# One streaming trunk layer on Trainium2: first weight tiles repacked, one small load issued elsewhere, three weight splits and two operand splits re-ordered

## The chip, the cores and the metric

The kernel runs on one core of a Trainium2 chip. The metric is the device time of one execution in microseconds (us). The kernel before takes 1087.67 us, the median of three runs (1087.66 to 1087.76). In the text a difference of 1 us is therefore about 0.09%.

## The reference, cut to what matters

One layer of a streaming encoder serves 512 new tokens (a prompt chunk) and 64 tokens of a running stream at once, 1024 features wide. Three blocks each add to `x`, and a last norm follows:

```python
x += mixer(rmsnorm(x))        # gated delta net (4 heads) and gated linear attention, merged by sigmoid gates, then w_o
x += cross_attn(rmsnorm(x))   # 4 heads of 256, into 256 memory tokens, then w_mo
x += conv_ffn(rmsnorm(x))     # up 1024 -> 2 x 2816, causal conv of width 3, SiLU gate, down
y  = rmsnorm(x)
```

The change touches four places of this: the first projections of the mixer (`q`, `k`, `v` of head 0, each 1024 -> 128, out of the normed `x`, whose per-feature gain is a vector), the product with `w_o` at the mixer's end, the attention output of the last memory head (`softmax(q k^T) v`), and the load of that gain vector. Everything is computed in float32 accuracy.

## The kernel before, in words

**Layout.** Features stand on the 128 partitions and tokens along the free axis: `x` is eight tiles of 128 x 576 (512 and 64 tokens side by side), and a weight tile of 1024 x 128 is one 128 x 1024 tile in the on-chip memory, eight 128 x 128 blocks behind each other.

**Accuracy by two halves.** TensorE takes operands in a rounded format (`fp32r`). Each operand is therefore split into a rounded high part and the rounded remainder, named `xh`, `xl` for the normed `x`, `ach`, `acl` or `hl` for other activations, and two tiles or halves named `w` for a weight. A product is three passes: high x high, weight high x remainder, weight remainder x high. `mm3` emits these for one 128 x 128 block, two matmuls each (256 and 320 tokens, in two PSUM banks `sm`): six matmuls for each block.

**Two ways to split a weight.** The raw weight comes by DMA into a tile `wr` on SyncE's queue. *With the subtraction*: ScalarE casts it to the high part (CAST), and VectorE or GpSimd subtracts the high part from the raw weight (TENSOR_TENSOR w<-wr,w). *Summed* (`split_summed`, L644): ScalarE writes the negated rounded weight into the place of the remainder (ACTIVATE with scale -1) and the high part (CAST), and then a DMA issued by GpSimd adds the raw weight onto the negated one. That DMA reads the raw weight a second time from HBM (`w<-wt`), or, where the weight is a sum of blocks formed on the chip, from that sum's tile `ws` (`w<-ws`).

**Products by sums of blocks.** For `w_o` two neighbouring output tiles form a pair (`WPAIRS`, four pairs, named by their first tile m = 0, 2, 4, 6). Each pair is done with seven products of sums of blocks: P1, P2, Q4, Q5, Q6, P3, Q7. `emit_product` (L651) loads the raw tiles with P1, forms the sums with `total` on VectorE or GpSimd (tiles `ws`), and splits each sum; its line `summed = ...` says which of the products take the summed way. `products` (L1645) emits the matmuls, `product_order` gives their order: pair by pair, with Q4 of a pair put behind P1 and Q5 of the next. The matmuls of a product come as eight with the weight's high part and then four with its remainder (128 x 288 each). `wo_finish` adds a finished bank to the tiles of `x` (SCALAR_TENSOR_TENSOR x<-sm,x on VectorE), and only then is that bank free for the product that accumulates into it next: Q5 and P3 share one bank, and P3 follows Q5 by one product.

**What sets the order.** All of this is written by one Python program. The main generator (`main`, L1689) emits the matmuls in order; other chains (norms, gates, attention heads) are generators beside it. A planner (`Driver`, L251) gives each instruction of the other engines a start time from costs per element (`FIXED`, `PACE`), keeps them in a heap, and `flush` (L289) emits them in the order of the planned times; the call stands in line 292, so that nearly every instruction has that line in the profile. Each engine then works through its own list in order and waits on semaphores. `load` plans a DMA of SyncE's queue, `accumulate` one of GpSimd. A chain that yields a list of tiles goes on when these are planned to be ready; one that yields a tuple of keys waits for other chains. One change in the planned times can so move rows in other places of the lists.

**The start.** SyncE issues the first eight numbers per partition of the gain vector (`vec`, 4 KB) and then tiles of `x` and halves of two raw weight tiles in turn (`WPART`, L760: which half follows which tile of `x`). The first two raw tiles hold `q` and `k` of head 0, packed so that the first holds both for the first four blocks. ScalarE makes `xh` and the weights' high parts, VectorE `xl` and the remainders. TensorE meanwhile runs eleven matmuls on constants (`warm`), then the blocks of `q` and `k`: q of block k and k of block k-1 in each step of the loop over `first2`. Then follow 32 matmuls with `w0` (gates; `sm<-x,w` in the profile), `v` of head 0 with a weight tile of its own, loaded after the others, and `za` (the gate of head 0). Among these are the sum of squares for the norm (`sm<-keep,acc`); from it GpSimd makes the factor `rt`, VectorE the diagonal tiles `dg`, TensorE spreads them (`sm<-dg,onesr`), ScalarE copies the result to `rbc`, VectorE multiplies with it (`ba<-sm,rbc`), and TensorE goes on with `sm<-cst,ba`.

**The attention heads.** `c_att` (L1527) emits one memory head: scores, softmax, transposes of the probabilities (`pth`, `ptl`), and two value products j = 0, 1 of 128 features each (banks `sm<-pth,kvh`). After each of them ScalarE copies the banks to `ao`, and `hl2` splits it into `ach` (ScalarE) and `acl` (VectorE). The output product `mo` of the first two tiles starts with heads 0 to 2, and takes head 3 as soon as its split parts are there.

Of the kernel before, what the change touches and what calls it, by code (L numbers as in the profile page):

```python
# [250 lines left out]
class Driver:  # L251
# [129 lines left out]

    def load(self, out, in_):
        cost = self.FIXED["D"] + free(out) * self.PACE["D"]
        start = self.place("D", max(self.ready_at(out), self.latest(self.seen, out)) + 2.2, cost)
        self.mark(self.wrote, start + cost, [out])
        self.put(start - 2.2, [(self.sync.dma_start, (out, in_), {})])

# [116 lines left out]
def tile_trunk(ctx, tc, xT, memT, wt, wd, vec, cst, w0, wgate, st_gdn, st_conv, st_gla, st_ffn, ckT, cv,  # L504
# [19 lines left out]
    def nm(s):  # L524
        cnt[0] += 1
        return f"{s}{cnt[0]}"
# [30 lines left out]
    def big():  # L557
        return Pair(sm(), sm())
# [41 lines left out]
    def make(i):  # L600
        fn = unmade.pop(i, None)
        if fn is not None:
            fn()
# [47 lines left out]
    def emit_product(i, at, pair, prod):  # L651
# [35 lines left out]
        h, lo = w[:, 0:n], w[:, 512:512 + n]  # L687
        summed = prod in ("P1", "P2", "Q4") or prod == "Q5" and n > 256 and pair[0][0] not in ("wo", "dn")

# [47 lines left out]


    ones_r = cp.tile([P, 128], F32R, name="onesr")
    G.memset(f(ones_r), 1.0)  # L740
# [8 lines left out]

    vec_t = cp.tile([P, NV], F32, name="vec")  # L750
    keep_t = cp.tile([P, 256], F32, name="keep")
    mbc_t = cp.tile([P, 256], F32, name="mbc")
    cst_t = small_tile([P, NM - 256], F32, tag="cst", name="cst", bufs=1)
    DMA(vec_t[:, 0:8], vec[:, 0:8])
    x = []
    raws = [wp.tile([P, 1024], F32, tag="raw", name=nm("wr"), bufs=RAWB) for _ in range(2)]
    for t_ in raws:
        keep(drv.rotate("raw", RAWB, t_))

    WPART = {0: (0, 0, 512), 2: (0, 512, 1024), 3: (1, 0, 512), 5: (1, 512, 1024)}  # L760
    for k in range(KT):
# [765 lines left out]
    def c_att(hd):  # L1527
# [51 lines left out]
        for j in range(2):  # L1579
# [10 lines left out]
            for c, reg in ((slice(0, TP), pp), (slice(TP, T), p64[:, 0:64])):  # L1590
                A.copy(o[:, c], reg)
            yield [o]
            ao[2 * hd + j] = hl2(o)
            os_.append(o)
            yield
        mops[hd] = {p: cut(ao[2 * hd + i], N1) for i, p in enumerate(("P1", "P2"))}
# [17 lines left out]
    def hl2(src, new=None):  # L1614
        h, lo = [(new or slot)(s, F32R) for s in ("ach", "acl")]
        parts2(h[:, 0:T], lo[:, 0:T], src[:, 0:T])
        return h[:, 0:T], lo[:, 0:T]
# [71 lines left out]
    def main():  # L1689
        acc = slot("acc")  # L1690
        xg = []
        for i in range(2):
            wready[i] = (w_tile()[:], w_tile()[:])
# [39 lines left out]
        drop(*(t_[:] for t_ in raws))  # L1733
        emit_weight(2)
        make(2)
        DMA(wg_t, wgate)
        DMA(cst_in, st_conv)
        xs = xs_of(xg)
        b0 = []
        (wh0, wl0), (wh1, wl1) = weight("q", 0, False), weight("k", 0, True, True)  # L1740
        first2 = [big(), big()]
        for k in range(KT + 1):
            for i, ps in enumerate(first2):
                j = k - i
                if 0 <= j < KT:
                    wh, wl = (wh0, wl0) if j < 4 else (wh1, wl1)
                    mm3([(ps[:, 0, 0:256], slice(0, 256)), (ps[:, 1, 0:320], slice(256, T))], wh, wl, *xs[j], 2 * (j % 4) + i, j == 0, j == KT - 1)
        raw_u = [conv_raw(ps, V.tensor_copy) for ps in first2]
        for k in range(4, KT):
# [24 lines left out]

        yield from tile_proj("v", 0, xs, b0)
        u0 = conv_raw(b0[0], A.copy)
        yield from tile_proj("za", 0, xs, b0)
        z0 = slot("z")
        for i, o in pieces(b0[1], z0):
            A.copy(o, i)  # L1780
# [711 lines left out]
def pack_inputs(inp):  # L2492
# [13 lines left out]
    for (kind, idx), i in WIDX.items():  # L2506
# [13 lines left out]
        wt[i] = kp(w)  # L2520
    wt[0:2] = wt[0:2].reshape(2, P, 2, 4, P).transpose(2, 1, 3, 0, 4).reshape(2, P, 1024)
    wd = a["w_down"][0].reshape(NJ, P, 8, P)[sum(PARTK, [])].transpose(2, 1, 0, 3).reshape(8, P, NJ * P)
# [65 lines left out]
```

## Time and profile before

| what | value |
|---|---|
| median of the runs | 1087.67 us (1087.66 to 1087.76) |
| the profiled execution's own time | 1090.06 us |
| its span in the trace | 1088.3 us |
| TensorE busy | 1077.5 us, 99% of the span |
| VectorE, ScalarE, GpSimd busy | 749.4, 705.9, 363.3 us |
| moved by DMA | 172.00 MB, mean 158 GB/s |
| weights added by DMA (`w<-wt`, `w<-ws`) | 153 and 27 of 256 to 512 KB |

The trace comes from one execution, whose own time is 2.39 us above the median of the runs; its span lies 1.76 us below that own time. In the rows, PE is TensorE, PEld its weight loads, DVE VectorE, ACT ScalarE, POOL GpSimd, SP SyncE with its DMA queue. A row of the timeline gives start, duration, engine, output and inputs, and in brackets the idle time just before and what ended it. Buffer numbers are left out of these names. TensorE's matmuls are pipelined, so that each lasts longer than the distance to the next; the distance is what counts. PEclk is the clock that was granted to TensorE, 1.00 being full.

### The profile page before, as it was taken

The numbers are of one execution on the slowest core, as the hardware profiler recorded it, in microseconds if no ns is written. First come the engines' busy times: TensorE is split into PE (matmuls) and PEld (weight loads), VectorE is DVE, ScalarE is ACT, GpSimd is POOL, SyncE is SP. The second block draws the span as 40 slices with busy tenths as digits, with TensorE's granted clock in tenths as the row PEclk, the third lists the DMA queues.
The fourth block names the chain that finished last, engine by engine and source line by source line (L and its number), as shares of the span: only waits on it lengthen the run. The fifth ranks groups of instructions, "written<-read, shape, count | busy, mean of one in ns | idle before, by whom it ended". The sixth has DMA issues, their size and how long they took to land.

```text
span 1088.3 us, 21600 instructions
## 1 busy us (share of the span) xinstructions
PE 1077.5 (99%) x8278; PEld 1045.7 (96%) x8278; DVE 749.4 (69%) x1460; ACT 705.9 (65%) x1404; POOL 363.3 (33%) x578
## 2 busy tenths in 40 slices
PE   9999999999999999999999999999999999999997
PEld 7999989998988999999999999999999999999997
DVE  6566844776757586887735766667877776778565
ACT  6675637464647568566755668768876776677645
POOL 1243216134524433123410125444333333332224
PEclk9999999999999999999999999999999999999999
DMA  9666344354136889678684258777788688778934
GB/s 295 145 143 162 70 110 114 76 123 122 43 78 130 213 213 188 246 222 211 174 221 146 49 124 195 175 166 150 166 195 196 146 213 188 168 172 184 201 77 112
DMA packets 68039, 172.00 MB, mean 158 GB/s; under 512 B 7904, under 2 KB 14176, under 8 KB 67936
## 3 DMA queue, kind: packets, MB, share of 16 engines
q0 software_dynamic: 30672, 71.84, 38.2%
q1 hardware_dynamic: 36976, 98.26, 27.7%
q8 instruction: 65, 1.06, 0.4%
q10 hardware_dynamic: 288, 0.52, 0.1%
q14 instruction: 38, 0.31, 0.1%
HBM read 158.15 MB, written 5.37 MB: 150 GB/s over the span
## 4 chain that ended last, share of the span: by engine, by line
PE 97%; DVE 1%; ACT 1%; DMA 0%; issue 0%; SPq 0%; ACTq 0%; DVEq 0%
PE sm L292 97%; DMA x<-xT 0%; DVE ql L292 0%; ACT w L292 0%; DVE w L292 0%; DVE acl L292 0%; DVE ws L292 0%; ACT ach L292 0%; SPq L292 0%; ACT ao L292 0%; DVE q L292 0%; DVE xl L292 0%; ACT xh L292 0%; DVE yo L292 0%; DVE x L292 0%
## 5 line engine op out<-in xcount | busy, mean ns | idle before, releaser
L292 PE MATMUL sm<-xh,w 128*128 128x290 f32 (+3 forms) x2304 | 446.3, 300 | 0.4 <-ACT xh L292 0.3
L292 PEld LDWEIGHTS sm<-xh,w 128*128 128x128 f32 x2304 | 357.2, 189 | 5.4 <-issue 1.7
L292 PE MATMUL sm<-xl,w 128*128 128x290 f32 (+3 forms) x1152 | 270.7, 296 | 0.5 <-DVE xl L292 0.5
L292 POOL DMA_DIRECT2D w<-wt x153 | 135.4, 898 | 372.4 <-ACT w L292 277.4
L292 PE MATMUL sm<-ach,w 128*128 128x256 f32 (+1 forms) x1216 | 230.9, 295 | 2.2 <-DVE x L292 1.7
L292 PEld LDWEIGHTS sm<-xl,w 128*128 128x128 f32 x1152 | 200.9, 189 | 1.0 <-DVE xl L292 1.0
L292 PEld LDWEIGHTS sm<-ach,w 128*128 128x128 f32 x1216 | 189.9, 188 | 3.0 <-ACT w L292 1.9
L292 ACT CAST w<-wr 128x512 fp32r<-128x512 f32 (+5 forms) x207 | 158.7, 769 | 20.8 <-PE sm L292 17.8
L292 ACT ACTIVATE w<-wr 128x512 fp32r<-128x512 f32 (+5 forms) x186 | 142.8, 769 | 20.4 <-PE sm L292 18.7
L292 PE MATMUL sm<-acl,w 128*128 128x256 f32 (+1 forms) x608 | 146.3, 295 | 0.3 <-DVE acl L292 0.3
L292 ACT CAST w<-ws 128x512 fp32r<-128x512 f32 (+1 forms) x132 | 78.4, 603 | 46.8 <-DVE ws L292 26.2
L292 PEld LDWEIGHTS sm<-acl,w 128*128 128x128 f32 x608 | 107.4, 188 | 0.5 <-DVE acl L292 0.5
L292 DVE TENSOR_TENSOR w<-ws,w 128x512 fp32r<-128x512 f32 (+1 forms) x104 | 76.1, 740 | 19.9 <-ACT w L292 17.7
L292 DVE SCALAR_TENSOR_TENSOR fc<-fu,vec,fc 128x578 f32<-128x578 f32 x88 | 70.4, 815 | 3.0 <-ACT fc L292 2.9
L292 PE MATMUL sm<-sh,w 128*128 128x290 f32 x288 | 61.2, 297 | 0.0
L292 DVE TENSOR_TENSOR x<-x,sm 128x320 f32<-128x320 f32 (+3 forms) x95 | 38.7, 437 | 31.4 <-PE sm L292 31.0
L292 POOL DMA_DIRECT2D w<-wd x33 | 29.0, 898 | 64.8 <-ACT w L292 57.9
L292 ACT ACTIVATE fc<-fu,vec 128x578 f32<-128x578 f32 x44 | 38.1, 871 | 17.0 <-POOL fu L292 16.4
L292 PEld LDWEIGHTS sm<-sh,w 128*128 128x128 f32 x288 | 47.5, 189 | 0.0
L292 DVE TENSOR_TENSOR ws<-ws,wr 128x512 f32<-128x512 f32 (+1 forms) x64 | 44.1, 690 | 1.1
L292 PE MATMUL sm<-oh,w 128*128 128x256 f32 (+1 forms) x256 | 44.7, 295 | 0.0
L292 POOL DMA_DIRECT2D w<-ws x27 | 23.6, 873 | 50.4 <-ACT w L292 49.9
(388 smaller groups left out, 1958.1 us busy)
## 6 DMA issues: line engine op xcount, KB each, us to landing
wr<-wt SPq DMA_DIRECT2D x130, 512.0 KB, 5.8
w<-wt POOLq DMA_DIRECT2D x52, 512.0 KB, 6.5
w<-wt POOLq DMA_DIRECT2D x101, 256.0 KB, 6.3
w<-ws POOLq DMA_DIRECT2D x27, 256.0 KB, 5.7
x<-xT SPq DMA_DIRECT2D x16, 288.0 KB, 6.1
wr<-wd SPq DMA_DIRECT2D x8, 448.0 KB, 5.9
w<-wd POOLq DMA_DIRECT2D x8, 448.0 KB, 7.1
wr<-wt SPq DMA_DIRECT2D x12, 256.0 KB, 3.8
```

What stands on the lines that cost most here:

```text
L292: fn(*args, **kw)
```

## The change

It has four parts.

1. `load` takes an issuer. The load of `vec[:, 0:8]` is issued by ScalarE's queue as its first instruction (ahead of its table load), no longer as the first of SyncE's queue.
2. `q`, `k` and `v` of head 0 share the first three raw tiles. They are packed block by block (q, k, v of block 0, then of block 1, and so on: 24 blocks in three tiles), and arrive in six halves behind tiles 0, 1, 2, 3, 5 and 6 of `x`. For each tile of `x` TensorE does the block of q, of k and of v. The own load and split of v's weight is gone (its summed split had an accumulating DMA, which goes with it), and the next weights (`za`) are fetched after these loops. The `w0` matmuls, the sum of squares and `za` follow directly; v's banks are copied by ScalarE.
3. `emit_product` takes the summed way also for Q5 of the pairs m = 2, 4, 6 of `w_o`. These three remainders are no longer subtracted by VectorE or GpSimd, but made by a second ScalarE instruction and an accumulating DMA out of the tile `ws`.
4. In head 3 of the attention the two value products are both emitted, and copied to `ao`, before either output is split by `hl2`.

```diff
-    def load(self, out, in_):
+    def load(self, out, in_, issuer=None):
...
-        self.put(start - 2.2, [(self.sync.dma_start, (out, in_), {})])
+        self.put(start - 2.2, [((issuer or self.sync).dma_start, (out, in_), {})])
...
-        summed = prod in ("P1", "P2", "Q4") or prod == "Q5" and n > 256 and pair[0][0] not in ("wo", "dn")
+        summed = prod in ("P1", "P2", "Q4") or prod == "Q5" and n > 256 and (pair[0][0] not in ("wo", "dn") or pair[0][0] == "wo" and pair[0][1])
...
+    vec_t = cp.tile([P, NV], F32, name="vec")
+    DMA(vec_t[:, 0:8], vec[:, 0:8], nc.scalar)
...
-    vec_t = cp.tile([P, NV], F32, name="vec")
...
-    DMA(vec_t[:, 0:8], vec[:, 0:8])
...
-    raws = [wp.tile([P, 1024], F32, tag="raw", name=nm("wr"), bufs=RAWB) for _ in range(2)]
+    raws = [wp.tile([P, 1024], F32, tag="raw", name=nm("wr"), bufs=RAWB) for _ in range(3)]
...
-    WPART = {0: (0, 0, 512), 2: (0, 512, 1024), 3: (1, 0, 512), 5: (1, 512, 1024)}
+    WPART = {k: (n // 2, 512 * (n % 2), 512 * (n % 2) + 512) for n, k in enumerate((0, 1, 2, 3, 5, 6))}
...
-            yield [o]
-            ao[2 * hd + j] = hl2(o)
             os_.append(o)
+            if not (hd == 3) or j:
+                yield [o]
+            for i in (range(2) if j and (hd == 3) else () if (hd == 3) else (j,)):
+                ao[2 * hd + i] = hl2(os_[i])
...
-        for i in range(2):
+        for i in range(3):
             wready[i] = (w_tile()[:], w_tile()[:])
...
-        emit_weight(2)
-        make(2)
...
-        (wh0, wl0), (wh1, wl1) = weight("q", 0, False), weight("k", 0, True, True)
-        first2 = [big(), big()]
-        for k in range(KT + 1):
-            for i, ps in enumerate(first2):
-                j = k - i
-                if 0 <= j < KT:
-                    wh, wl = (wh0, wl0) if j < 4 else (wh1, wl1)
-                    mm3([(ps[:, 0, 0:256], slice(0, 256)), (ps[:, 1, 0:320], slice(256, T))], wh, wl, *xs[j], 2 * (j % 4) + i, j == 0, j == KT - 1)
-        raw_u = [conv_raw(ps, V.tensor_copy) for ps in first2]
+        ws = [weight(kd, 0, False, i) for i, kd in enumerate("qkv")]
+        first3 = [big() for _ in range(3)]
+        for k in range(KT):
+            for i, ps in enumerate(first3):
+                n, b = divmod(3 * k + i, 8)
+                mm3([(ps[:, 0, 0:256], slice(0, 256)), (ps[:, 1, 0:320], slice(256, T))], *ws[n], *xs[k], b, k == 0, k == KT - 1)
+        raw_u = [conv_raw(ps, copy) for ps, copy in zip(first3, (V.tensor_copy, V.tensor_copy, A.copy))]
+        fetch(3)
...
-        yield from tile_proj("v", 0, xs, b0)
-        u0 = conv_raw(b0[0], A.copy)
+        u0 = raw_u[2]
...
-    wt[0:2] = wt[0:2].reshape(2, P, 2, 4, P).transpose(2, 1, 3, 0, 4).reshape(2, P, 1024)
+    wt[0:3] = wt[0:3].reshape(3, P, KT, P).transpose(2, 0, 1, 3).reshape(3, 8, P, P).transpose(0, 2, 1, 3).reshape(3, P, 1024)
```

TensorE has the same 7340 rows before and after; they stand in another order in three places. At the start, rows 6 to 11 of its list before (sm39/sm40 are q's banks, sm41/sm42 k's; xh17 is tile 0 of the normed x, xh19 tile 1; w13, w14 the first weight's two parts):

```order
L292 MATMUL sm39_131<-xh17_109,w14_106 128x256
L292 MATMUL sm40_132<-xh17_109,w14_106 128x320
L292 MATMUL sm39_131<-xh19_111,w13_105 128x256
L292 MATMUL sm40_132<-xh19_111,w13_105 128x320
L292 MATMUL sm39_131<-xl20_112,w13_105 128x256
L292 MATMUL sm40_132<-xl20_112,w13_105 128x320
```

and with the change (xh20 is tile 0 now; sm43/sm44 are v's banks):

```order
L292 MATMUL sm39_131<-xh20_112,w15_107 128x256
L292 MATMUL sm40_132<-xh20_112,w15_107 128x320
L292 MATMUL sm41_133<-xh20_112,w14_106 128x256
L292 MATMUL sm42_134<-xh20_112,w14_106 128x320
L292 MATMUL sm41_133<-xl21_113,w14_106 128x256
L292 MATMUL sm42_134<-xl21_113,w14_106 128x320
L292 MATMUL sm41_133<-xh20_112,w15_107 128x256
L292 MATMUL sm42_134<-xh20_112,w15_107 128x320
L292 MATMUL sm43_135<-xh20_112,w14_106 128x256
L292 MATMUL sm44_136<-xh20_112,w14_106 128x320
```

Where q went on to tile 1 after six matmuls, q, k and v now all use tile 0 first, 18 matmuls.

In the product with `w_o`, GpSimd's list while pair 0 is being finished, before (w1169 is P1 of pair 2, w1178 Q4 of pair 0, w1182 P2 of pair 2, w1190 and w1191 P1 and Q5 of pair 4; w1176 is Q5 of pair 2):

```order
L292 DMA w1169_6121<-wt 128x512
L292 DMA w1178_6182<-wt 128x512
L292 DMA w1182_6202<-wt 128x512
L292 TENSOR_TENSOR ws1185_6223<-ws1180_6184,wr1167_6119 128x512
L292 DMA w1190_6304<-wt 128x512
L292 DMA w1196_6325<-wt 128x512
L292 DMA w1200_6354<-wt 128x512
```

and with the change:

```order
L292 DMA w1169_6123<-wt 128x512
L292 DMA w1178_6184<-wt 128x512
L292 DMA w1182_6204<-wt 128x512
L292 DMA w1176_6182<-ws1177_6183 128x512
L292 DMA w1196_6328<-wt 128x512
L292 DMA w1190_6287<-wt 128x512
L292 DMA w1200_6354<-wt 128x512
L292 DMA w1191_6313<-ws1192_6314 128x512
```

The addition ws1185 has left GpSimd, and two accumulating DMAs for Q5 weights (w1176, w1191) have come in behind others. VectorE's list in the same place, before (w1179 is Q6 of pair 2, ws1185 the sum for its P3; the two rows behind it add finished banks to `x`, the second of them Q5 of pair 0):

```order
L292 TENSOR_TENSOR ws1180_6184<-ws1177_6181,wr1167_6119 128x512
L292 TENSOR_TENSOR w1176_6180<-ws1177_6181,w1176_6180 128x512
L292 TENSOR_TENSOR w1179_6183<-ws1180_6184,w1179_6183 128x512
L292 SCALAR_TENSOR_TENSOR x1113_5839<-sm1181_6185,x1113_5839 128x288
L292 SCALAR_TENSOR_TENSOR x1114_5840<-sm1183_6203,x1114_5840 128x288
```

and with the change:

```order
L292 TENSOR_TENSOR ws1180_6186<-ws1177_6183,wr1167_6121 128x512
L292 SCALAR_TENSOR_TENSOR x1113_5841<-sm1181_6187,x1113_5841 128x288
L292 SCALAR_TENSOR_TENSOR x1114_5842<-sm1183_6205,x1114_5842 128x288
L292 TENSOR_TENSOR w1179_6185<-ws1180_6186,w1179_6185 128x512
L292 TENSOR_TENSOR ws1185_6225<-ws1180_6186,wr1167_6121 128x512
```

The subtraction for w1176 is gone, the two additions to `x` stand ahead of w1179, and ws1185 has come over from GpSimd.

At the end of head 3, TensorE's rows behind its second value product, before (ach1510 and ach1515 are the first and second output's high parts, acl1511 and acl1516 the remainders):

```order
L292 MATMUL sm1513_8125<-pst1500_7983,cvr1403_7551 128x64
L292 MATMUL sm1491_7952<-ach1510_8113,w1433_7686 128x256
L292 MATMUL sm1492_7953<-ach1510_8113,w1433_7686 128x320
L292 MATMUL sm1491_7952<-acl1511_8114,w1433_7686 128x256
L292 MATMUL sm1492_7953<-acl1511_8114,w1433_7686 128x320
L292 MATMUL sm1491_7952<-ach1510_8113,w1434_7687 128x256
L292 MATMUL sm1492_7953<-ach1510_8113,w1434_7687 128x320
L292 MATMUL sm1491_7952<-ach1515_8145,w1433_7686 128x256
```

and with the change (ach1471 is an output of head 2; ach1513 is now head 3's first output; its second, ach1515, follows after one more row):

```order
L292 MATMUL sm1511_8119<-pst1500_7996,cvr1408_7579 128x64
L292 MATMUL sm1505_8043<-ach1471_7885,w1460_7828 128x256
L292 MATMUL sm1506_8044<-ach1471_7885,w1460_7828 128x320
L292 MATMUL sm1505_8043<-acl1472_7886,w1460_7828 128x256
L292 MATMUL sm1506_8044<-acl1472_7886,w1460_7828 128x320
L292 MATMUL sm1505_8043<-ach1471_7885,w1461_7829 128x256
L292 MATMUL sm1506_8044<-ach1471_7885,w1461_7829 128x320
L292 MATMUL sm1491_7956<-ach1513_8147,w1435_7695 128x256
L292 MATMUL sm1492_7957<-ach1513_8147,w1435_7695 128x320
L292 MATMUL sm1491_7956<-acl1514_8148,w1435_7695 128x256
L292 MATMUL sm1492_7957<-acl1514_8148,w1435_7695 128x320
L292 MATMUL sm1491_7956<-ach1513_8147,w1436_7696 128x256
```

Twelve matmuls instead of six now stand between the second value product and the first use of its output. Earlier in the same stretch, six matmuls of `mv` (`sm<-w,mh`) have moved ahead of head 3's scores (`sm<-kvh,ql`).

More of the change, by code (lines that the diff above doesn't have):

```diff
@@ L1773, in main @@
         drv.spawn(c_first())
-        yield from tile_proj("v", 0, xs, b0)
-        u0 = conv_raw(b0[0], A.copy)
+        u0 = raw_u[2]
         yield from tile_proj("za", 0, xs, b0)
         z0 = slot("z")
-        for i, o in pieces(b0[1], z0):
+        for i, o in pieces(b0[0], z0):
             A.copy(o, i)
```

## The prediction

> **What bounds the kernel now.** I read the page's engine totals and the chain that ended last first.
>
> ```profile
> PE 1077.5 (99%) x8278; PEld 1045.7 (96%) x8278; DVE 749.4 (69%) x1460; ACT 705.9 (65%) x1404; POOL 363.3 (33%) x578
> PE 97%; DVE 1%; ACT 1%; DMA 0%; issue 0%; SPq 0%; ACTq 0%; DVEq 0%
> ```
>
> TensorE is busy for 99% of the span, and the change leaves it the same matmuls. Time can only come from its waits and from stretches at a lower clock. The timeline of PE shows where these are at the start.
>
> ```profile
> 1.00 4.97 PE L292 MATMUL warm<-onesr 128*128 128x512 f32 x11 [1.00 <-POOL onesr L292]
> 5.88 0.88 PE L292 MATMUL sm<-xh,w 128*128 128x256 f32 x2
> 7.07 0.41 PE L292 MATMUL sm<-xl,w 128*128 128x320 f32 x1 [0.19 <-DVE xl L292]
> 8.06 0.53 PE L292 MATMUL sm<-xh,w 128*128 128x256 f32 x2 [0.31 <-ACT xh L292]
> 8.91 0.67 PE L292 MATMUL sm<-xl,w 128*128 128x256 f32 x2 [0.32 <-DVE xl L292]
> 9.38 1.16 PE L292 MATMUL sm<-xh,w 128*128 128x256 f32 x4
> 10.82 1.16 PE L292 MATMUL sm<-xh,w 128*128 128x256 f32 x4
> 13.99 0.69 PE L292 MATMUL sm<-xh,w 128*128 128x256 f32 x4
> 20.33 0.70 PE L292 MATMUL sm<-xh,w 128*128 128x256 f32 x4
> 22.28 2.15 PE L292 MATMUL sm<-x,w 128*32 128x256 f32 x32
> ```
>
> From 13.99 to 20.33 lie 48 matmuls: 0.132 us each. From 9.38 to 10.82 six take 1.44, 0.24 each. The 96 matmuls of q and k, begun at 5.88, would end at 18.55 at 0.132; they end at 22.28. The start loses 3.73 us, by waits for xh and xl and by a slow stretch, which the view by windows shows, with a later one for comparison:
>
> ```profile
> 5.73:9.14 3.41, 2.51 (x11) 1.45 (x11) 2.25 (x4) 2.48 (x5) 0.00 (x0) 1.00 1.02 374
> 9.14:12.55 3.41, 3.41 (x16) 3.41 (x16) 3.40 (x6) 3.16 (x6) 0.00 (x0) 0.50 1.04 393
> 486.96:490.37 3.41, 1.67 (x13) 1.46 (x13) 3.26 (x7) 0.81 (x2) 1.22 (x1) 1.00 1.04 248
> ```
>
> The columns are the window, its length, the busy time of PE, PEld, DVE, ACT and POOL, PEclk, DMA share and GB/s. Behind a first window with PE busy for 2.51 of 3.41 us the clock was 0.50 for one window; DMA was saturated in both (1.02, 1.04).
>
> **Shared first tiles.** A tile of x (295 KB) and half a weight tile (262 KB) arrive in 557/393 = 1.4 us. q and k gave PE 12 x 0.132 = 1.6 us of work per tile of x; with v it is 2.4. So from the second tile on the feed runs ahead and the waits at 8.06 and 8.91 go. The first wait stays, since xl's second part comes at its old distance behind the first weight: 0.19 idle, with the refilling of the pipeline 0.3 (the matmul behind it lasts 0.41 instead of 0.28 to 0.31). Under the old order PE went on to tile 1 after six matmuls (0.8 us at full clock) and met the feed there; now 18 matmuls (2.4) stand before the first use of tile 1, and tile 1 was ready at 8.06 and 8.91, against 5.88 + 0.3 + 2.4 = 8.6 for its xh and 0.3 more for its xl. Both land 0.4 earlier as well (below). With PE filled, I expect full clock in 9.14 to 12.55. [...] Gain by rows: 3.73 - 0.3 = 3.4 us.
>
> What follows must keep up, since w0, the sum of squares and `za` now come 3.4 us earlier:
>
> ```profile
> 28.16 1.15 PE L292 MATMUL sm<-keep,acc 128*128 128x1 f32 x10
> 29.80 1.20 POOL L292 TENSOR_TENSOR rt<-rin,mhalf 128x5 f32<-128x5 f32 x1 [5.80 <-DVE rin L292]
> 34.09 0.97 PE L292 MATMUL sm<-dg,onesr 128*128 128x512 f32 x4
> 36.46 0.71 ACT L292 COPY rbc<-sm 128x512 f32<-128x512 f32 x2
> 37.09 0.82 DVE L292 TENSOR_TENSOR ba<-sm,rbc 128x256 f32<-128x256 f32 x2 [4.16 <-ACT rbc L292]
> 39.31 1.17 PE L292 MATMUL sm<-cst,ba 128*128 128x8 f32 x10
> ```
>
> The last row is the point by which both orders have done the same work on TensorE: q, k, v, w0, the sum of squares, `za` and the diagonals. Unstalled, it is due at 39.31 - 3.4 = 35.9. With 144 matmuls of q, k, v (19.0 us) the loops end at 5.88 + 0.3 + 19.0 = 25.2, w0 2.1 and the sum of squares 1.1 later: 28.4. From there to dg the chain runs over rin, rt (1.20 on GpSimd) and VectorE; before, TensorE met dg at 34.09, 4.8 behind the end of the sum at 29.3, and did not wait. Now the diagonals stand 36 matmuls of `za` behind the sum (28.4 + 4.8 = 33.2, end 34.1), the same distance, so no wait there. rbc and ba take 0.71 + 0.82 and some 0.2 of handing over: 35.8. That just fits, if ScalarE is free for rbc; behind ba stand the `wg` matmuls and then the next weight's, so that whatever ba is late, TensorE loses. I take 0.3 off (0 to 1.8, the latter if rbc waits for a weight copy as long as it did before: 36.46 against 35.06). **Start: -3.1.**
>
> **The small load.** It leaves SyncE's queue:
>
> ```profile
> 0.74 0.39 SPq L292 DMA_DIRECT2D vec<-vec  x1
> ```
>
> Every x and weight lands about 0.4 us earlier. The first matmul does not move, because the warm ones end at 5.88; the rest is feed that already runs ahead. ScalarE's issue of it (0.4, as on SyncE) delays its table load, and both are over before x has landed, for which it waits. Alone it is worth 0 to 0.4, hidden by the warm matmuls; I take 0. Without the warm ones it would be the 0.4.
>
> **Q5 of w_o.** The longest wait is here: the chain of waits, the timelines of POOL and PE, and the page's group of subtractions.
>
> ```profile
> 487.18 1.55 DVE w L292
> 488.73 0.74 DVE x L292 x2
> 486.45 1.73 POOL L292 TENSOR_TENSOR ws<-ws,wr 128x512 f32<-128x512 f32 x1
> 489.61 0.37 PE L292 MATMUL sm<-ach,w 128*128 128x288 f32 x1 [1.75 <-DVE x L292]
> L292 DVE TENSOR_TENSOR w<-ws,w 128x512 fp32r<-128x512 f32 (+1 forms) x104 | 76.1, 740 | 19.9 <-ACT w L292 17.7
> ```
>
> P3 of pair 0 waits until VectorE has added Q5's bank to x; that stands behind a subtraction of 1.55 us, usually 0.74, while GpSimd adds beside it. GpSimd's addition (1.73) covers just that time. With the change the additions stand ahead of the subtraction and GpSimd adds nothing there; behind the chain VectorE is then late with w1179 and ws1185 only, 0.7 each, whose products come later. The wait goes: 1.75 and 0.15 of refilling, 1.9 us.
>
> But the remainder of pair 2's Q5 now hangs on a DMA.
>
> ```profile
> 485.70 0.61 ACT L292 CAST w<-ws 128x512 fp32r<-128x512 f32 x1
> 482.97 1.75 POOL L292 DMA_DIRECT2D w<-wt  x2 [6.12 <-DVE kraw L292]
> 485.57 0.86 POOL L292 DMA_DIRECT2D w<-wt  x1 [0.85 <-ACT w L292]
> DMA to landing us min/median/max: 7.5/7.5/7.5
> DMA to landing us min/median/max: 9.1/9.1/9.1
> w<-ws POOLq DMA_DIRECT2D x27, 256.0 KB, 5.7
> 495.53 0.82 PE L292 MATMUL sm<-ach,w 128*128 128x288 f32 x5
> ```
>
> The two landing lines are those of the DMAs at 482.97 and 485.57: they land at 490.5 and 494.7, the third two after the first, 2.1 us apart. ScalarE now does two instructions of 0.6 from 485.70, so the new DMA is issued at 486.9, behind these three. It is needed where the row at 495.53 stands (Q5's four remainder matmuls), less the 1.9: 493.6. From below, 5.7 after 486.9 is 492.6, no wait. From above, one more spacing behind 494.7 is 496.8, a wait of 3.2. The nearer row is the neighbour on the same queue; as one load of x moves ahead (295 KB, 0.8 us), I take 496.0, a wait of 2.4. [...] Behind Q5's remainder on TensorE stand Q4 of pair 0 and all the rest, so the whole wait counts; on GpSimd's queue stand the DMAs for Q4 and P1 of the next pairs, needed a pair later. Pairs 4 and 6 have the same DMA, issued behind ScalarE's split of P2, but with fewer in the queue ahead; I take 0.3 together (0 to 6.4, each as late as the upper end of pair 2). **w_o: -1.9 + 2.4 + 0.3 = +0.8**, ends -1.9 and +7.7.
>
> **Head 3.** Three waits, by PE's timeline and the chain:
>
> ```profile
> 620.70 0.38 PE L292 MATMUL sm<-kvh,ql 128*128 128x256 f32 x1 [0.26 <-DVE ql L292]
> 643.97 0.53 PE L292 MATMUL sm<-ach,w 128*128 128x256 f32 x2 [0.48 <-ACT ach L292]
> 644.76 0.54 PE L292 MATMUL sm<-acl,w 128*128 128x256 f32 x2 [0.26 <-DVE acl L292]
> 642.51 0.71 ACT ao L292 x2
> 643.25 0.68 ACT ach L292
> 643.95 0.77 DVE acl L292
> ```
>
> Six more matmuls (0.7 us) now cover ql: its 0.26 goes. Behind the second value product 12 matmuls (1.6) cover ao and ach (1.4): 0.48 goes. acl is ready 0.8 later, and needed 0.3 later: 0.4 stays where 0.26 was. Value products and transposes of other heads have moved among the matmuls of `mq`; no wait stood there, and I count them at nothing, at worst one more wait like the 0.26. **-0.6** (+0.3 to -1.0).
>
> **Sum**: -3.1 + 0 + 0.8 - 0.6 = -2.9. The profiled execution took 1090.06, 2.39 above the median; 1087.67 - 2.9 = **1084.8**. The likeliest case's own range is 1083.4 to 1086.2.
>
> **Rivals.** (a) *The Q5 DMAs land in time.* For it: the median of 5.7. Against: the three queued ahead. Then -2.9 - 2.4 - 0.3 = -5.6: 1082.1. (b) *The new wait costs a slow window.* PE then idles 2.4 of a 3.41 us window, more than the 1.74 that cost nothing at 486.96; a window at 0.50 does half its work and adds 1.7: 1086.5. The same 1.7 is lost if the window behind 9.14 is slow again, for a reason other than PE's waits. (c) *The norm's chain holds the start.* ScalarE copies weights ahead of rbc, and the chain in front of it has no slack left; 1.5 more is lost (the upper end of 1.8 above, less the 0.3 in the sum): 1086.3. (d) *Slower: the queue of accumulating DMAs.* All three Q5 remainders are as late as the upper end, 3.2 each: 9.6 instead of 2.7, so -2.9 + 6.9 = +4.0: 1091.7. It decides from a total wait of 2.9 + 2.7 + 2.2, 7.8 us. Against it: only at pair 2 do three others stand ahead. (e) That the change doesn't do what it says: the lists show each part done; only the small load may move nothing, which is in the sum.
>
> **How the numbers follow.** Forecast 0.46, (a) 0.12, (b) 0.20, (c) 0.13, (d) 0.09. A measurement of this kernel tells about 0.2% from no change, 2.2 us, so faster means under 1085.5 and slower over 1089.85. Faster: four fifths of the forecast, (a), and a little of (b) and (c): 0.52. Slower: (d), 0.09. Same: 0.39. The range takes in (a), (b), (c) and a mild (d): 1082.0 to 1088.2.
>
> **What would show it.** Right: no PEclk under 1.00 behind 5.73; `sm<-x,w` at about 25.2 behind three products; no gap before P3 of pair 0; a gap of about 2.4 before Q5's remainder matmuls of pair 2, ended by a DMA; one small gap at head 3. Wrong: a window at 0.50 in the first 16 us or behind 494, idle time before `sm<-cst,ba` over 0.5, or gaps of more than 1 us at pairs 4 and 6.

## The result, and the profile after

The changed kernel takes **1093.12 us** (median of six runs, 1091.98 to 1093.34), the kernel before 1087.77 beside it on the same chip: ratio 1.0045, 95% interval 1.0032 to 1.0058. It is slower by 5.35 us where the prediction had 2.9 us faster, and 1093.12 lies outside the range of 1082.0 to 1088.2. The profiled execution took 1092.82 with a span of 1091.0, so it stands for the median.

The page of the changed kernel: engine totals, the chain that ended last, and the group of the matmuls that use `ach`.

```profile
PE 1077.5 (99%) x8278; PEld 1046.9 (96%) x8278; DVE 748.9 (69%) x1461; ACT 706.7 (65%) x1407; POOL 361.2 (33%) x578
PE 95%; DMA 2%; issue 1%; DVE 1%; ACT 0%; POOL 0%; POOLq 0%
L292 PE MATMUL sm<-ach,w 128*128 128x256 f32 (+1 forms) x1216 | 233.1, 297 | 6.0 <-DMA w<-ws 4.6
```

A DMA has come onto the chain (2%, before 0%), and one group of matmuls waits 4.6 us for `w<-ws`, the accumulating DMAs out of the tile of sums. TensorE's busy time is the same as before to the digit. I take that for a coincidence: at the start a slow stretch of the profiled execution before has gone, and in `w_o` a new one has come.

**The start** of the changed kernel, TensorE's timeline and then its windows (window, length, busy time of PE, PEld, DVE, ACT and POOL, PEclk, DMA share, GB/s):

```profile
5.66 0.43 PE L292 MATMUL sm<-xh,w 128*128 128x256 f32 x2
25.25 2.15 PE L292 MATMUL sm<-x,w 128*32 128x256 f32 x32
35.99 1.17 PE L292 MATMUL sm<-cst,ba 128*128 128x8 f32 x10
```

```profile
5.73:9.14 3.41, 3.27 (x25) 3.03 (x24) 2.60 (x5) 2.59 (x4) 0.00 (x0) 1.00 1.00 355
9.14:12.55 3.41, 3.41 (x28) 3.41 (x28) 3.41 (x6) 3.22 (x5) 0.00 (x0) 1.00 1.05 401
```

`sm<-x,w` stands at 25.25 (forecast 25.2), `sm<-cst,ba` at 35.99 (forecast 35.9), and the clock is full in both windows. Against the profiled execution before (39.31) the start gained 3.32.

**In `w_o`**, TensorE's timeline around pair 2 and pair 4:

```profile
487.69 1.75 PE L292 MATMUL sm<-hl,w 128*128 128x288 f32 x12
495.10 1.57 PE L292 MATMUL sm<-ach,w 128*128 128x288 f32 x5 [4.60 <-DMA w<-ws]
498.14 1.41 PE L292 MATMUL sm<-ach,w 128*128 128x288 f32 x5
517.16 0.37 PE L292 MATMUL sm<-ach,w 128*128 128x288 f32 x1 [1.41 <-DVE x L292]
```

P3 of pair 0 no longer waits. But Q5's remainder matmuls of pair 2 wait 4.60 for their DMA, and behind it five matmuls last 1.57 and 1.41 where they lasted 0.82. The windows show why:

```profile
486.93:490.34 3.41, 3.41 (x27) 3.33 (x26) 2.48 (x5) 2.70 (x6) 0.68 (x1) 1.00 1.11 283
490.34:493.75 3.41, 0.16 (x2) 0.00 (x0) 0.00 (x0) 0.58 (x2) 1.04 (x2) 0.96 1.05 307
493.75:497.16 3.41, 2.06 (x8) 2.06 (x9) 0.46 (x1) 0.00 (x0) 0.00 (x0) 0.50 1.08 291
497.16:500.57 3.41, 3.41 (x16) 3.41 (x16) 1.19 (x3) 1.18 (x3) 0.25 (x1) 0.54 0.26 49
500.57:503.98 3.41, 3.41 (x28) 3.41 (x27) 2.61 (x5) 2.67 (x5) 2.68 (x3) 1.00 0.61 96
```

TensorE stands still from 490.50 to 495.10. Read in slices of half a microsecond, the granted clock falls at 493.5, still inside the gap, and is full again from 500.3; in between it is 0.50, and the fourth window has 16 matmuls where the fifth has 28. The DMA engines are full (1.05 to 1.11) in the first three windows, through the wait and 2 us beyond it, and at 0.26 in the fourth.

The chain of waits of this stretch says what is waited for:

```profile
483.41 11.65 DMA w<-ws
495.06 0.04 issue
495.10 9.51 PE sm L292 x52
...
515.97 0.68 DVE w L292
516.64 0.38 DVE x L292
517.16 2.90 PE sm L292 x20
```

The DMA is issued at 483.41, nearly as forecast (486.9 less the 3.3 that the start gained is 483.6), and lands 11.65 us later. The second wait, at pair 4, is of the old kind in a new place: VectorE's subtractions stand ahead of its addition to `x`, and GpSimd adds beside them. By the count of the matmuls the one that waits is the first of Q7 of pair 4; it was P3 at pair 0, the only pair in which P3 follows Q5 by one product. VectorE's timeline, then GpSimd's:

```profile
488.29 0.69 DVE L292 TENSOR_TENSOR w<-ws,w 128x512 fp32r<-128x512 f32 x1 [0.39 <-ACT w L292]
513.92 2.73 DVE L292 TENSOR_TENSOR w<-ws,w 128x512 fp32r<-128x512 f32 x2 [0.41 <-DMA w<-wt]
```

```profile
513.71 1.77 POOL L292 TENSOR_TENSOR acc<-acc,sq 128x576 f32<-128x576 f32 x1
```

A subtraction alone takes 0.69 (488.29). Of the two from 513.92 the first holds VectorE until 515.97, where the chain has the second: 2.05 us, up to 0.5 behind the end of GpSimd's addition (515.48). VectorE also began it late, after 0.41 of waiting for an accumulating DMA (`w<-wt`).

That the addition holds the subtraction up is read from the two standing side by side, here (2.05 us beside 1.77) and at pair 0 before (1.55 beside 1.73), with 0.69 for a subtraction alone. How it does so the trace does not show.

**Head 3** has one row left with a wait, in TensorE's timeline:

```profile
647.06 0.53 PE L292 MATMUL sm<-acl,w 128*128 128x256 f32 x2 [0.22 <-DVE acl L292]
```

### The profile page after: what moved, and what is told of

Read it like the earlier page. It is cut to its first block, busy times and chain, and to the rows that moved or that the text cites. A ratio compares the mean times of both kernels' runs of the same rounds, so it can differ in the third digit from the quotient of the medians.

```text
span 1091.0 us, 21590 instructions
## 1 busy us (share of the span) xinstructions
PE 1077.5 (99%) x8278; PEld 1046.9 (96%) x8278; DVE 748.9 (69%) x1461; ACT 706.7 (65%) x1407; POOL 361.2 (33%) x578
## 3 DMA queue, kind: packets, MB, share of 16 engines
HBM read 157.63 MB, written 5.37 MB: 149 GB/s over the span
## 4 chain that ended last, share of the span: by engine, by line
PE 95%; DMA 2%; issue 1%; DVE 1%; ACT 0%; POOL 0%; POOLq 0%
PE sm L292 95%; DMA w<-ws 1%; DMA w<-wt 1%; DMA vec<-vec 0%; DVE ql L292 0%; POOL w L292 0%; POOL acc L292 0%; DVE acl L292 0%; ACT ao L292 0%; ACT ach L292 0%; DVE w L292 0%; DVE x L292 0%; DVE yo L292 0%; DVE q L292 0%; ACT sq L292 0%
## 5 line engine op out<-in xcount | busy, mean ns | idle before, releaser
L292 DVE TENSOR_TENSOR w<-ws,w 128x512 fp32r<-128x512 f32 (+1 forms) x101 | 72.1, 722 | 18.9 <-ACT w L292 16.6
L292 POOL DMA_DIRECT2D w<-ws x30 | 26.7, 891 | 51.8 <-ACT w L292 51.0
```

The costliest lines, as they stand in the source:

```text
L292: fn(*args, **kw)
```

## The experiments

Each run stands beside runs of the kernel before on the same chip, whose medians were 1088.07, 1087.88 and 1087.96 us on the three chips used; a difference to the kernel before is to its median there.

### The kernel before once more

No edit. It asks whether the profiled execution, 2.39 above the median, stands for the others.

> The kernel before, unchanged, once more beside itself. Theory A (the profiled execution of before, 2.4 us above the median of its runs, holds a slow window at the start that most executions do not have): own time of this profile near 1087.7 us, and no or a shorter stretch at granted clock 0.50 behind 9 us. Theory B (that window is part of every execution): again a window of 3.4 us at 0.50 behind 9 us. Both: same time as before within 0.2%.

Measured: 1087.92, ratio 0.9999 (0.9990 to 1.0009); its profiled execution took 1088.08. TensorE's timeline and the windows:

```profile
6.08 0.88 PE L292 MATMUL sm<-xh,w 128*128 128x256 f32 x2 [0.69 <-ACT w L292]
37.23 0.95 PE L292 MATMUL sm<-cst,ba 128*128 128x8 f32 x8
```

```profile
5.73:9.14 3.41, 2.64 (x14) 1.98 (x15) 2.60 (x4) 2.87 (x6) 0.00 (x0) 1.00 1.00 372
9.14:12.55 3.41, 3.41 (x28) 3.41 (x27) 3.40 (x6) 3.29 (x5) 0.00 (x0) 1.00 1.04 392
```

There is no window at 0.50, and `sm<-cst,ba` stands at 37.23, 2.08 earlier than in the execution on which the prediction was built. The waits are not quite the same either: the second tile of x lands 4.5 us after its issue at 2.1 where it took 5.1, and TensorE waits 0.69 for the first weight and 0.20 for xl, where it waited 0.19, 0.31 and 0.32 for xl, xh and xl. Of the 2.08, half a window, 1.7, is the slow clock; the rest lies in these waits. So nearly all of the offset of 2.39 is the start of that one execution. The run with Q5 alone (below), which has the start of the kernel before, bears this out: `sm<-cst,ba` at 37.18, clock 1.00 from 5.73 to 12.55. Against 37.23 the change gains 37.23 - 35.99 = 1.24 at the start.

### The change without its Q5 part, and the Q5 part alone

```diff
-        summed = ... or prod == "Q5" and n > 256 and (pair[0][0] not in ("wo", "dn") or pair[0][0] == "wo" and pair[0][1])
+        summed = ... or prod == "Q5" and n > 256 and pair[0][0] not in ("wo", "dn")
```

> The change with its third part undone (Q5 of w_o is split with the subtraction, as before). Theory A (the accumulating DMAs of Q5 cost all of the loss, the start and head 3 gain): faster than before by 1.5 to 4.2 us (start 0.7 to 3.3, head 3 0.85), 1083.5 to 1086.3 us; no wait on DMA w<-ws near 491, the old wait of 1.75 us on DVE x back. Theory B (what the start wins is given back later): within 0.9 us of before.

The other way round, the kernel before with this line of the change alone:

> The kernel before with the third part alone (Q5 of pairs 2, 4, 6 summed). Theory A: slower than before by 6 to 7 us, about 1094 us: a wait of about 4.8 us for DMA w<-ws at pair 2, half clock behind it (2.6 us lost), a wait of 1.4 to 1.6 us behind DVE x at pair 4, less the 1.9 us that go. Theory B (the wait at pair 2 is so long only because the start came earlier and moved the loads against TensorE): a wait of 2.4 us as forecast, slower by 0.5 to 2 us.

Measured: without Q5 1086.70, ratio 0.9987 (0.9979 to 0.9996); Q5 alone 1095.01, ratio 1.0063 (1.0049 to 1.0077). The timeline of the first, and of the second:

```profile
486.30 0.37 PE L292 MATMUL sm<-ach,w 128*128 128x288 f32 x1 [1.73 <-DVE x L292]
```

```profile
496.14 1.57 PE L292 MATMUL sm<-ach,w 128*128 128x288 f32 x5 [4.59 <-DMA w<-ws]
518.44 0.37 PE L292 MATMUL sm<-ach,w 128*128 128x288 f32 x1 [1.42 <-DVE x L292]
```

Q5 costs 6.9 alone, as theory A had it, and 6.7 on top of the rest (5.35 + 1.37). With it the DMA wait and pair 4's wait come, without it the old wait of 1.7 comes back. The rest of the change gains 1.37, which leaves the time 0.4 above theory A's range.

Where the 6.7 lie is seen by setting the same matmul of both traces against each other (with Q5 less without): +0.1 ahead of P3 of pair 0, -1.85 behind it, +5.33 at 504, +6.98 at 522, +6.1 to 6.6 from 650 on. So: -1.96 for the old wait, +7.18 at pair 2 (4.60 of waiting, 2.58 of half clock and refilling), +1.65 at pair 4.

### The start alone, and its two parts apart

First parts 1 and 2 of the change without the others:

> The kernel before with parts one and two alone (small load on ScalarE's queue, q, k and v sharing the first tiles). Theory A: faster than before by 0.7 to 3.3 us, depending on how often before has its slow window; TensorE at full clock from 5.7 us on, w0 matmuls at 25.2 us. Theory B: no difference beyond 0.5 us.

Then the kernel before with part 1 alone (`load` with an issuer, `vec` first on ScalarE's queue), and with part 2 alone (the three shared tiles, `vec` still on SyncE's queue):

> The kernel before with the small load alone issued from ScalarE. Theory A, the feed is not what the start waits for until the first tiles are done: `sm<-cst,ba` stays at 37.2 and the time at 1087.9. Rival B, every tile of x is 0.4 us earlier and TensorE, which meets the feed at tiles 0 and 1, passes it on: 36.8 and 1087.5.

> The kernel before with q, k and v of head 0 on shared first tiles, and the small load left on SyncE's queue. Theory A, the sharing makes the whole gain of the start: `sm<-cst,ba` at 35.9 as with both parts, time 1087.1. Rival B, the sharing needs the earlier feed: 36.3 or later, a wait of more than 0.3 ahead of one of the first tiles, time 1087.5 or more.

Measured: both parts 1087.17, ratio 0.9993 (0.9985 to 1.0002); the load alone 1087.37, ratio 0.9993 (0.9984 to 1.0002); the sharing alone 1088.07, ratio 1.0001 (0.9992 to 1.0009). By time none is told from no change; the timelines tell more. The first row is that of both parts, then the load, then the sharing:

```profile
35.89 1.17 PE L292 MATMUL sm<-cst,ba 128*128 128x8 f32 x10
```

```profile
36.81 1.17 PE L292 MATMUL sm<-cst,ba 128*128 128x8 f32 x10
```

```profile
36.66 1.16 PE L292 MATMUL sm<-cst,ba 128*128 128x8 f32 x10
```

Against 37.23 the load stands 0.42 earlier, the sharing 0.57, both together 1.34: both times rival B, though the wait of more than 0.3 that the second asks for at a first tile did not show (the longest is 0.19). These are single executions, and the start varies: with both parts `sm<-cst,ba` stands at 35.87 to 36.24 in eight traces, and at 36.70 in the ninth, the run with pair 4 alone. The feed goes with it. With the load on SyncE's queue ScalarE begins the first weight's cast at 5.13 to 5.45 (four traces), with the load moved at 4.36 to 4.73 (nine traces) and at 5.21 in that run of 36.70. So the earlier feed is worth something, on top of the sharing more than alone; how much in the usual execution, one trace of each doesn't tell.

### Which pair costs

The same line, with Q5 summed in pair 2 only (`== 2` behind `pair[0][1]`), then in pair 4 only (`== 4`):

> The change with the summed Q5 in pair 2 alone (pairs 4 and 6 by subtraction, as before). TensorE's list is that of the kernel without any summed Q5 (1086.7 us). Theory A (the DMA of pair 2 stands last of four on GpSimd's queue and is the whole loss, with the slow clock that follows the wait): a wait of 4.4 to 5.2 us before the row's remainder matmuls, 0.50 of the clock behind it, time 1091 to 1092.5. Theory B (the three together cost it, by their load on the DMA engines): less than half, under 1089.5.

> The summed Q5 in pair 4 alone. Theory A: no wait for its DMA over 0.5 us, since only one other stands ahead of it on the queue, the old wait of 1.75 us on DVE x stays, time 1086.2 to 1087.5. Theory B (each such DMA lands too late): a wait over 2 us at pair 4, 1089 or more.

Measured: pair 2 alone 1093.25, ratio 1.0048 (1.0033 to 1.0063); pair 4 alone 1086.38, ratio 0.9987 (0.9978 to 0.9996). The timeline of the first:

```profile
495.28 1.57 PE L292 MATMUL sm<-ach,w 128*128 128x288 f32 x5 [4.49 <-DMA w<-ws]
521.51 0.40 PE L292 MATMUL sm<-ach,w 128*128 128x288 f32 x1 [0.52 <-DVE x L292]
```

and of the second:

```profile
487.00 0.37 PE L292 MATMUL sm<-ach,w 128*128 128x288 f32 x1 [1.73 <-DVE x L292]
```

With pair 2 alone the whole loss is there: 5.37 over the kernel before, where the change has 5.35. The wait is in theory A's range, the time 0.75 above it. Pair 4's DMA is waited for by nobody; only the old wait is there. Neither run has the wait of 1.4 at pair 4.

### Pair 2 with a shorter queue

The change with Q5 summed in pair 2 only, and the remainder of P2 of that pair subtracted, so that two accumulating DMAs stand ahead of Q5's and not three:

```diff
-        summed = prod in ("P1", "P2", "Q4") or prod == "Q5" and ...
+        summed = (prod in ("P1", "P2", "Q4") and not (prod == "P2" and pair[0] == ("wo", 2))) or prod == "Q5" and ... == 2)
```

> As the run with pair 2 alone, but P2 of pair 2 is split by subtraction, so that two accumulating DMAs, not three, stand ahead of Q5's. Theory A: it lands 2 to 3 us earlier; a wait of 1.5 to 3 us instead of 4.8, too short for a window at 0.50 behind it; with the old wait gone 1086.3 to 1088.3. Theory B (the transfer is slow because it reads on-chip memory and shares with SyncE's loads, wherever it stands in the queue): a wait of over 4 us again, 1091 or more.

Measured: 1086.34, ratio 0.9987 (0.9978 to 0.9996), 6.91 less than with the full queue. Its timeline, and what the view of the tile says of Q5's DMA, issued at 483.50 (the wait after it is TensorE's):

```profile
485.48 0.37 PE L292 MATMUL sm<-ach,w 128*128 128x288 f32 x1 [0.69 <-DVE x L292]
491.78 0.93 PE L292 MATMUL sm<-ach,w 128*128 128x288 f32 x5 [0.24 <-DMA w<-ws]
```

```profile
  PE sm L292: 0.2, 1
DMA to landing us min/median/max: 8.2/8.2/8.2
```

The same DMA, issued at nearly the same time, lands 8.2 us after its issue, instead of 11.5 in the run with pair 2 alone and 11.65 in the change. One DMA less ahead of it decides, more than theory A thought (a wait of 1.5 to 3), and with the wait the half clock goes too: the clock is 1.00 from 486 to 501. Whether it is the place in the queue or the 256 KB less to move, this run doesn't separate.

### The old wait by another way

The change with Q5 subtracted as before, and the sums of `w_o` formed by VectorE only, so that GpSimd adds nothing beside P3's wait (`if pair[0][0] == "mo"` for `in ("wo", "mo")` in `total`):

> The change without any summed Q5, and in addition the sums of the blocks of w_o formed on VectorE only, never on GpSimd. Theory A (the old wait of 1.75 us is the collision of VectorE's subtraction with GpSimd's addition beside it): the subtraction takes 0.7 instead of 1.55 us and the wait before P3 of pair 0 falls below 0.5, 1084.8 to 1085.5. Theory B (the wait is VectorE's list being full there; one more addition on it makes it worse): the wait stays over 1.2 us, 1086.4 to 1087.5.

Measured: 1087.51, ratio 0.9996 (0.9987 to 1.0005). Theory A's time was missed:

```profile
485.56 0.37 PE L292 MATMUL sm<-ach,w 128*128 128x288 f32 x1 [0.87 <-DVE x L292]
520.55 0.37 PE L292 MATMUL sm<-ach,w 128*128 128x288 f32 x1 [1.32 <-DVE x L292]
```

The collision is the cause of half the wait: VectorE's two subtractions ahead of the addition to x take 1.53 us instead of 2.38 in the run without Q5, and the wait falls from 1.73 to 0.87, between the two theories. The other wait, 1.32, comes at pair 6, ahead of Q7 by the count of the matmuls. There two subtractions of 128x1024 for later weights (3.59 us from 516.45) now stand in a row ahead of the addition to x, which in the run without Q5 has its place between them; so the order moved, and that VectorE's one addition more is the cause is not shown. Q5's DMA relieves VectorE at pair 0 more: in the change the wait there is gone. Only pair 2's DMA comes too late.

### Filling the gap

Twenty more matmuls in the gap at pair 2, all other lists as in the change. The first matmul of the product is repeated with `start=True`, which begins the bank anew each time.

```diff
                 PE.matmul(o, wh[:, 128 * i:128 * i + 128], h, start=start and i == 0, stop=False, skip_group_check=True)
+                if pair[0] == ("wo", 2) and prod == "Q5" and i == 0:
+                    PE.put(PE.now - 0.001, 20 * [(nc.tensor.matmul, (o, wh[:, 0:128], h), dict(start=True, stop=False, skip_group_check=True))])
```

> The change, with twenty idle matmuls put into the gap ahead of the remainder of pair 2's Q5: the first matmul of that product is repeated (each time it starts the bank anew, so the sum is the same). Every other list stays as in the change. Theory A, the half clock behind the gap comes from TensorE standing still for 4.6 us: 20 x 0.13 = 2.6 us of the gap are filled, about 2.0 us of waiting for the DMA are left, no window at 0.50 follows, and the time is 1093.1 - 2.6 = 1090.5. Rival B, the clock falls there for another reason (the saturated DMA, or a state of its own): the gap is filled as well, 0.50 still shows behind 493, and the time stays at 1093.1.

Measured: 1091.54 (1090.14 to 1093.20, five runs), ratio 1.0034 (1.0022 to 1.0047); the profiled execution took 1092.86. Its timeline and windows:

```profile
495.38 1.39 PE L292 MATMUL sm<-ach,w 128*128 128x288 f32 x5 [2.36 <-DMA w<-ws]
```

```profile
490.34:493.75 3.41, 2.68 (x21) 2.44 (x19) 0.00 (x0) 0.42 (x1) 0.89 (x2) 1.00 1.07 317
493.75:497.16 3.41, 1.78 (x8) 1.79 (x9) 0.46 (x1) 0.00 (x0) 0.00 (x0) 0.77 1.09 281
497.16:500.57 3.41, 3.41 (x21) 3.41 (x20) 1.20 (x3) 1.19 (x3) 0.26 (x1) 0.73 0.19 34
```

The gap shrinks to 2.36, as expected. In this execution the half clock is shorter, one window's worth in two (0.77, 0.73) for two at 0.50 and 0.54, but it has not gone: in finer slices it falls at 495.6, just behind the gap, and is full again from 499.0, 3.4 us where the change had 6.8. By its time this execution saved nothing. The median is 1.6 lower, between theory A's 1090.5 and the rival's 1093.1, and the five runs reach from the one to the other. That speaks for standing still as part of the cause; that it alone decides is not shown. Of the rival's two causes, saturated DMA alone is not enough: at the start of the changed kernel the DMA share was 1.05 from 9.14 to 12.55 and the clock 1.00.

### Both put together

The change with all three Q5 sums, and P2 of pair 2 subtracted (the line above without `== 2`):

> The change, with the remainder of P2 of pair 2 subtracted by VectorE or GpSimd instead of added by a DMA; all three Q5 remainders stay with a DMA. Theory A, what costs is only pair 2's place in GpSimd's DMA queue: with two DMAs ahead the wait at pair 2 is 0.2 as in the run with pair 2 alone, pairs 4 and 6 wait for no DMA, and the gains of pair 2 and pair 4 add up: 1086.7 - 0.4 - 0.3 = 1086.0. Rival B, with all three sums the work that VectorE and GpSimd have left still meets at pair 4: a wait of 1.4 for x there, 1087.5 or more.

Measured: **1085.50**, ratio 0.9979 (0.9971 to 0.9988), 2.46 less than before (the interval leaves out 1), and less than the changed kernel. Its timeline, and the view of Q5's DMA of pair 2 (issued at 483.12):

```profile
485.10 0.37 PE L292 MATMUL sm<-ach,w 128*128 128x288 f32 x1 [0.69 <-DVE x L292]
514.82 0.40 PE L292 MATMUL sm<-ach,w 128*128 128x288 f32 x1 [0.52 <-DVE x L292]
```

```profile
DMA to landing us min/median/max: 8.1/8.1/8.1
```

No matmul waits for a DMA in `w_o`, and both waits for x are small. It came out 0.5 below theory A's 1086.0. The wait of 1.4 at pair 4 is gone too, with all three Q5 still summed: it stood in the three runs that had all three and a late pair 2 (the change, Q5 alone, the filled gap) and in no other.

## Why the prediction was wrong

The parts were the right ones, and one of them had the wrong size: TensorE waited 4.6 us for a weight made by a DMA where 2.4 were forecast, and 2.6 us more went into the half clock behind it. The gain at the start was also too large.

**The start: mechanism right, and the gain taken from an execution that was not typical.** The steps forecast for the trace came: 25.25 for 25.2, 35.99 for 35.9, full clock, and no wait at `sm<-cst,ba`. But "-3.1" was summed from the profiled execution and then taken off the median, with the 2.39 between them as a plain offset. Of those 2.39, 2.08 were the slow window and the longer waits of that one start. The execution without the window lost only 1.65 there (37.23 against 39.31 less 3.73), and the runs gave -0.9 for parts 1 and 2, with an interval that takes in no change. This step alone was about 2.2 too good.

**The small load at 0: likely mis-sized.** In single traces it is worth 0.42 alone and 0.77 on top of the sharing (36.66 to 35.89); by the times it is not told from 0. The cover named, the warm matmuls, did not always hold: in the kernel before once more they ended at 5.38, and TensorE waited 0.69 for the first weight.

**P3's wait, -1.9: right** (-1.96).

**Q5 of pair 2, +2.4: the step that turned the sign.** This is the step that failed: the landing of Q5's DMA, and with it the wait. The issue was placed rightly (483.41), the need too (about 490.4). The landing was not. The forecast set it at 496.0 in the old trace, 492.7 in the new; the bounds were 489.3 and 493.5. It landed at 495.06. The upper end took one old spacing, 2.1, behind an unchanged P2, which was to land at 494.7 - 3.3 = 491.4. The view of the tile gives P2's landing after its issue at 482.37, and Q5's after 483.41:

```profile
DMA to landing us min/median/max: 10.2/10.2/10.2
DMA to landing us min/median/max: 11.6/11.6/11.6
```

So P2 itself landed at 492.6, 1.2 late, and Q5 2.5 behind it: 1.6 beyond the upper end. The three ahead were counted, but their landings were taken as fixed. They are not: the same DMA of P2 takes 8.9 to 9.2 us in the eight traces in which no Q5 DMA follows it (both of the kernel before, without Q5, the start and its two parts, pair 4 alone, sums on VectorE) and 10.1 to 10.5 in the four in which one does, a microsecond behind it (the change, Q5 alone, pair 2 alone, the filled gap). In these traces the newcomer goes with a delay of about 1 us for the one ahead of it, so these DMAs of the queue were not served one at a time to their end. That the DMA engines were full all along (1.05 to 1.11) fits it; how much of the delay is the loads on SyncE's queue was not tried. The run with the shorter queue shows that one DMA less is worth 3.3 us of landing (495.06 to 491.74).

VectorE's work is not seen to hold the DMA engines up here: from 490.34 to 493.75 VectorE was not busy at all (0.00) and the DMA share was 1.05, and in the window before, with VectorE busy for 2.48 of 3.41 us, it was 1.11.

**The clock behind the wait was a rival, and came with it.** Rival (b) put 1.7 on one slow window behind a wait of 2.4. With 4.6 of waiting it was two windows and 2.6 (5.2 us of work at half clock, from 495.10 to 500.3). Wait and clock together made +7.2 at pair 2 where the sum had 2.4.

The half clock lasted 6.8 us in the change (493.5 to 500.3) and 3.4 with the filled gap (495.6 to 499.0), as long as two of the windows above and one. In the change the clock fell 3.0 us into the gap. With the filled gap it fell although TensorE had stood still for only 2.36 us, while 1.75 in the kernel before (ahead of 489.61) were not followed by a lower clock. The busy share of one window does not settle it: 1.05 of 3.41 us (filled gap) and 2.51 (start of the kernel before) were followed by half clock, 1.67 (486.96) was not. What decides stays open.

**Pairs 4 and 6, +0.3: wrong in kind.** TensorE waited for no DMA there. Instead a collision of VectorE with GpSimd, which the prediction saw only at pair 0, came at pair 4: +1.65. GpSimd's part in it is another, the sum of squares (`acc<-acc,sq`) for the next norm. The words that VectorE "is then late with w1179 and ws1185 only" looked at the rows moved at pair 0 and not at what stands side by side later. With pair 2 in time it does not come.

**Head 3, -0.6: right in the main.** The run without Q5 lies 0.47 below the start alone; ach's wait has gone, 0.22 is left at acl where 0.4 was forecast. ql's wait has gone in the change, but in the run without Q5 it is still there (0.27), so the 0.47 is without it.

In sum: start -0.9 for -3.1, `w_o` +6.7 for +0.8, head 3 -0.5 for -0.6, which makes +5.3 for the measured +5.35. The sum closes because the 6.7 is itself a difference to the measured time; the run with Q5 alone gives 6.9 independently. Rival (d), the slower one, had the right queue, but asked for all three pairs to be late and left the clock out.

## What to carry to other kernels

A remainder made by a DMA spares VectorE a subtraction (0.69 us, for an ACTIVATE of 0.63 on ScalarE, at 482.49 in the change, and an issue of 0.86 on GpSimd) and is dear in time: here it landed 8.1 to 8.2 us after its issue with two DMAs just ahead on its queue, and 11.5 to 12.1 with three. So count the queue at its issue and let the earlier ones slip too, or shorten the queue where the need is near. Before a gain is summed from one profiled execution and taken off a median, ask whether the difference between the two is one of the very terms. A wait for a DMA of several microseconds on TensorE should be priced with the clock behind it, here more than half as much again (2.58 on 4.60).

## What the runs showed of the hardware

- The kernel before fell to half clock at 9.14 in one profiled execution and not in the other, with PE busy for 2.51 and 2.64 of the 3.41 us ahead. The waits were nearly the same in sum (0.82 and 0.89 us), so a single trace doesn't tell the clock behind them.
- One gap of 4.6 us brought two windows of half clock, 6.8 us from 3.0 us into the gap on, the second of them with PE busy throughout at the lower clock.
- The four accumulating DMAs of 256 KB on GpSimd's queue, issued within 3.7 us, landed 7.4, 9.1, 10.2 and 11.6 us after their issue.
- The third of them, without the fourth behind it, landed after 8.9 to 9.2 us (eight traces), with it after 10.1 to 10.5 (four traces).
- VectorE's subtraction of 128x512, 0.69 us alone, held VectorE for 1.55 and 2.05 us beside an addition on GpSimd of 1.73 and 1.77 us.
